# Value projection of a dilated-attention layer: from 384 columns a unit to 512 columns over several units

## The chip, the cores and the metric

The kernel runs on one core of one Trainium2 chip. The metric is the device time of one execution in microseconds (us). The median of three runs is 747.87 us (747.73 to 748.14).

## What is computed

A trunk of two layers on 256 tokens of 1024 features in float32: an even layer (neighbourhood attention and latent attention) with its MLP, then an odd layer with its MLP, and a final norm. The change lies in the odd layer's attention alone. Cut to that:

```python
def odd_mixer(xn, w_in, w_o, cos_f, sin_f):      # xn = rms_norm(x, norm_mix[layer])
    hcat = (xn @ w_in).reshape(b, s, 3, 3, 16, 64)   # group, q/k/v, head, dim
    q = apply_rope(hcat[:, :, :, 0], cos_f, sin_f)
    k = apply_rope(hcat[:, :, :, 1], cos_f, sin_f)
    v = hcat[:, :, :, 2]
    return dilated_attention(q, k, v) @ w_o
```

Each of 16 heads has three groups of queries, keys and values (windows of 128 at stride 1, 512 at stride 4, 2048 at stride 16). A softmax runs over each group, and the three outputs are weighted by their softmax denominators, which is the same as one softmax over all three together.

## The kernel before

**Layout.** A unit is a pair of heads; there are 8. Products keep float32 accuracy by splitting each operand into a high and a low part: `split` (L181, L182) makes the high part on ScalarE and the low part on VectorE, and `mm3` (L185 to L187) multiplies high by high, high by low and low by high. The normed input is kept as `pair` (high and low parts side by side) without the norm's factor rstd; that factor is multiplied in afterwards, into the values as they leave PSUM (L846 to L850) and into the rope tables for queries and keys (L989 to L991).

**Weights.** `specs` lists all weight chunks in the order of use. `weight()` hands out the next one and first calls `prefetch`, which issues loads up to four chunks ahead on SP's queue (L150) and splits up to two chunks ahead, in four pieces each. There are four buffers of raw chunks and three of split ones. The odd layer uses, per unit, three chunks of 2048 columns for queries and keys (`w_oqk`, in `QK_ORDER` 0, 2, 1) and two of 1536 for values (`w_ov`).

**PSUM.** Eight banks: four with the tag "acc" (products) and four with the tag "w" (scores, transposes, row products).

**Queries and keys** (`qk_steps`, L854). Each chunk makes two halves f of 128 columns; each half takes eight pairs of matmuls, one of 512 columns (L867) and one of 256 (L868), in two steps. A chunk is four steps, a unit twelve. What a half leaves in its bank is added up on VectorE (L874 with ScalarE's copy L873, or the reduce L876). `rope` then swaps quarters of the partitions, by DMA on SP's queue for chunks 0 and 2 and by four ScalarE copies (L885, L886) for chunk 1, and multiplies and adds on VectorE (L888 to L898). Chunk 0 gives q and k of the first group (`q0h`, `q0l`), chunk 2 the keys `k12` and chunk 1 the queries `q12` of the other two groups (L894).

**Values** (`value_steps`, L829). For one unit: two token tiles, each one bank of 384 columns, eight k-slices by three matmuls (L185 to L187, called from L844). The first 128 columns are the first group's and leave by VectorE (L846); the others leave by ScalarE in pieces of 64 x 128 (L849, L850), rearranged by tokens.

**Attention** (L912). `scores` fills four "w" banks (L194 for the first group, 16 small matmuls L925 for the others, which read `q12`) and runs the softmax (L934 to L938); `turn` transposes probabilities (L945) and copies them out (L947); `mix` multiplies them by the values (L955, L960) in two banks. `attend` (L974) gives eight steps: scores with the mix of the unit before, four turns, and empty ones.

**Order.** `weave(main, side)` (L196) calls the steps of one list and deals the other list's steps out among them. Tile then orders each engine's instructions from the program, before anything runs. In the opening (L980 to L992) unit 0's values are woven with the squares of x; then `rstd` follows (L244: column sums on TensorE, L239; power on GpSimd, L247), the diagonals of rstd (L258), the evacuations of the values, unit 0's queries and keys in two pieces, and between these pieces the row product (L265) that brings rstd to the rope tables. After that each unit's 12 query-key and 4 value steps are woven with the attention of the unit before. Unit 6's mix is dealt out at the end of unit 7's values (L1002), and unit 7's attention runs beside the output projection.

Of the kernel before, what the change touches and what calls it, by code (L numbers as in the profile page):

```python
# [16 lines left out]
F32 = mybir.dt.float32  # L17
# [6 lines left out]
P = 128  # L24
D = 1024
KT = D // P
# [14 lines left out]
NORM_PRIO = 300  # L41

QK_ORDER = (0, 2, 1)


@with_exitstack
def trunk(ctx, tc, a, out):
# [29 lines left out]
    def bank(tag):  # L77
        return ps.tile([P, 512], F32, tag=tag, name=tag)
# [51 lines left out]
    plan("w_uq", 2 * 768)  # L130
    plan("w_oe", 2 * D)
    plan_mlp(0)
    for u in range(8):
        ov = [(a["w_ov"][u, j], 4 * 384) for j in range(2)]
        oqk = [(a["w_oqk"][u, j], WCH) for j in QK_ORDER]
        specs.extend(oqk + ov if u else ov + oqk)
    plan("w_oo", 2 * D)
    plan_mlp(1)

# [667 lines left out]
    def odd(op, xT, s):  # L807
# [14 lines left out]
        def unit_tiles(u):  # L822
            d = {"k12": k12[u % 2]}
            for n, shape, dt in (("q0h", [P, 2, T], F32R), ("q0l", [P, 2, T], F32R), ("q12", [P, 2, T], F32),
                                 ("v0", [P, NT, P], F32), ("v12", [P, 4, P], F32)):
                d[n] = op.tile(shape, dt, tag=n, name=n, bufs=2)
            return d

        def value_steps(d):  # L829

            wt, acc = [], {}

            def gemm(i, half):
                if len(wt) <= half:
                    wt.append(weight())
                if half == 0:
                    acc[i] = bank("acc")
                pq = acc[i]
                wh, wl = wt[half]
                for k in range(4):  # L840
                    ws = slice(k * 384, k * 384 + 384)
                    kk = 4 * half + k
                    mm3(pq[:, 0:384], xh[:, kk, tok(i)], xl[:, kk, tok(i)], wh[:, ws], wl[:, ws], kk == 0, kk == KT - 1)
            def out(i):  # L844
                pq, ri = acc[i], column(r[0], i)
                nc.vector.tensor_scalar(d["v0"][:, i, :], pq[:, 0:P], ri, None, ALU.mult)  # L846
                for c in range(2):
                    rows = slice(64 * c, 64 * c + 64)
                    nc.scalar.activation(d["v12"][0:64, 2 * i + c, :], pq[rows, P:2 * P], AF.Copy, scale=ri[rows])  # L849
                    nc.scalar.activation(d["v12"][64:P, 2 * i + c, :], pq[rows, 2 * P:3 * P], AF.Copy, scale=ri[rows])  # L850

            return [lambda i=i, h=h: gemm(i, h) for i in range(NT) for h in range(2)], [lambda i=i: out(i) for i in range(NT)]

        def qk_steps(d):  # L854


            hold = {}

            def gemm(b, f, half):
                if f == 0 and half == 0:  # L860
                    hold["w"], hold["q"] = weight(), op.tile([P, 2, T], F32, tag="qk32", name="qk32", bufs=2)
                if half == 0:
                    hold["p"] = bank("acc")
                (wh, wl), pq, q32 = hold["w"], hold["p"], hold["q"]
                for k in range(4 * half, 4 * half + 4):
                    ws = slice((f * KT + k) * P, (f * KT + k + 1) * P)
# [12 lines left out]

            def rope(b, pq):  # L880

                sw, r1 = op.tile([P, 512], F32, tag="swap", name="sw", bufs=2), scratch([2, T], "r1")
                change = nc.scalar.copy if b == 1 else nc.sync.dma_start
                for r in range(0, P, 64):
                    change(sw[r:r + 32], pq[r + 32:r + 64])  # L885
                    change(sw[r + 32:r + 64], pq[r:r + 32])  # L886
                sw = sw.rearrange("p (f n) -> p f n", f=2)
                nc.vector.tensor_tensor(r1, pq.rearrange("p (f n) -> p f n", f=2), cosT.unsqueeze(1).broadcast_to([P, 2, T]), op=ALU.mult)  # L888
                nc.vector.tensor_tensor(sw, sw, sinT.unsqueeze(1).broadcast_to([P, 2, T]), op=ALU.mult)
                if b == 0:  # L890
                    nc.vector.tensor_tensor(r1, r1, sw, op=ALU.add)
                    split(d["q0h"], d["q0l"], r1)
                elif b == 1:
                    nc.vector.tensor_tensor(d["q12"], r1, sw, op=ALU.add)  # L894
                else:
                    for r in (0, 64):
                        cut = lambda z: z[r:r + 64].rearrange("p j (c n) -> p j c n", n=64)
                        nc.vector.tensor_tensor(d["k12"][r:r + 64, :, :, r:r + 64], cut(r1), cut(sw), op=ALU.add)  # L898

            return [lambda v=(b, f, h): gemm(*v) for b in QK_ORDER for f in range(2) for h in range(2)]  # L900

        def all_values(d, prio=0):
            g, o = value_steps(d)
            o = [lambda f=f: early(f) for f in o] if prio else o

            def early(f):
                with tc.high_priority(prio):
                    f()

            return [g[0], lambda: run_all([g[1], o[0]]), g[2], lambda: run_all([g[3], o[1]])]  # L910

        def attention(u, d):  # L912

# [34 lines left out]

            def mix(out_tag):
                pvo = [bank(out_tag) for _ in range(NT)]  # L950
                for i in range(NT):
                    for kk in range(NT):
                        for j in range(2):
                            cs = slice(64 * j, 64 * j + 64)
                            nc.tensor.matmul(pvo[i][cs, 0:P], d["v0"][:, kk, cs], turned[i, j][:, kk, :], start=kk == 0, stop=False)  # L955
                    for c in range(2):
                        qs = slice(64 * c, 64 * c + 64)
                        for j in range(2):
                            cs = slice(64 * j, 64 * j + 64)
                            nc.tensor.matmul(pvo[i][cs, qs], d["v12"][:, 2 * i + c, cs], turned[i, j][:, 2, qs], start=False, stop=c == 1)  # L960
                with tc.high_priority(NORM_PRIO):
                    for i in range(NT):
                        split(*(z[:, u % 4, tok(i)] for z in mixed[u // 4]), pvo[i][:, 0:P])
# [13 lines left out]
            done.append(mix)  # L977
            return [lambda: (scores(), before("acc")), nothing, nothing, t0, t1, nothing, t2, t3]

        d, nd = unit_tiles(0), unit_tiles(1)  # L980
        v0, v_out = value_steps(d)
        squares = square_steps(s)
        weave(v0[0::2] + v0[1::2], squares, 1)
        r = [rstd(s)]
        dg = [diagonal(r[0], t) for t in range(NT)]
        run_all(v_out)
        first = qk_steps(d)
        run_all(first[:2])
        row = as_row(dg)  # L989
        for z in (cosT, sinT):  # L990
            nc.vector.tensor_tensor(z, z, row, op=ALU.mult)  # L991
        run_all(first[2:])  # L992
        weave(qk_steps(nd) + all_values(nd), attend(0, d) + [nothing], 3)
        for u in range(2, 7):
            d, nd = nd, unit_tiles(u)
            weave(qk_steps(nd) + all_values(nd), attend(u - 1, d) + [nothing] * 2)

        d, nd = nd, unit_tiles(7)
        steps = attend(6, d)
        mix = done.pop()  # L1000
        weave(qk_steps(nd) + all_values(nd, NORM_PRIO), steps + [nothing, lambda: mix("w")])
        steps = attend(7, nd)  # L1002
        steps[0]()
        accs, wo = open_accs(), {}
        mix = done.pop()
# [52 lines left out]
def _layout(i):  # L1058
# [20 lines left out]
    d["w_ov"] = f(wo[:, :, 2].reshape(2, 4, P, 3, 8, P).transpose(4, 0, 2, 1, 3, 5).reshape(8, 2, P, 4 * 384))  # L1079
# [34 lines left out]
```

## Time and profile before

| what | value |
|---|---|
| median of three runs | 747.87 us |
| the profiled execution | 748.65 us |
| its span | 746.9 us |
| granted TensorE clock, mean | 0.997 |
| VectorE's split of the raw weights, 512 columns | x408, mean 687 ns |
| the same, 384 columns | x68, mean 553 ns |

The profile is of one execution, and its times are microseconds from the start of the span. Engines: PE is TensorE's matmuls and PEld its weight loads, DVE is VectorE, ACT ScalarE, POOL GpSimd, SP SyncE. L182 is line 182 of the kernel before. A matmul's modelled duration contains its way through the array, so the pitch from one start to the next tells more than the duration. The second layer's attention lies between about 294 and 553 us.

### The profile page before, as it was taken

The page shows a single profiled execution, that of the slowest core. Times are in us where ns is not written, and L with a number is a line of the kernel's source. Part 1 is how long each engine was busy: PE and PEld are TensorE (multiplying, and loading weights), DVE is VectorE, ACT ScalarE, POOL GpSimd, SP SyncE. Part 2 cuts the span into 40 slices and gives each one's busy share as a digit, 9 for nine tenths or more (in the row PEclk, how much of TensorE's full clock was granted, in tenths as well). Part 3 has the DMA queues.
Part 4 walks back from the last instruction along what each step waited for, and adds up shares of the span by engine and source line. Part 5 has one row for each costly group of instructions (what it writes and reads, how often), then busy time and mean ns, then how long its engine had stood idle before and what let it go on. Part 6 is the DMA issues. An engine that isn't in the chain of part 4 may idle for free.

```text
span 746.9 us, 12279 instructions
## 1 busy us (share of the span) xinstructions
PE 739.0 (99%) x4635; PEld 646.4 (87%) x4635; DVE 544.2 (73%) x1137; ACT 484.8 (65%) x1075; POOL 8.7 (1%) x20
## 2 busy tenths in 40 slices
PE   9999999999999999999999999999999999999996
PEld 6998998888888888889899899998998888888885
DVE  6778858766566666997888788888858765665664
ACT  6788967554554555677786877867856554554551
POOL 0100000000000001000000000000000000000000
PEclk9999999999999999999999999999999999999998
DMA  8763334464555545554645636445545555545501
GB/s 282 317 255 114 114 113 170 171 225 173 179 211 177 186 172 165 200 183 165 208 141 178 223 122 215 165 162 198 203 165 176 190 198 197 186 183 187 193 15 56
DMA packets 25163, 133.19 MB, mean 178 GB/s; under 512 B 3728, under 2 KB 4752, under 8 KB 12304
## 3 DMA queue, kind: packets, MB, share of 16 engines
q1 hardware_dynamic: 24960, 132.15, 50.1%
q8 instruction: 36, 0.59, 0.3%
q10 hardware_dynamic: 144, 0.26, 0.1%
q14 instruction: 23, 0.19, 0.1%
HBM read 127.16 MB, written 1.05 MB: 172 GB/s over the span
## 4 chain that ended last, share of the span: by engine, by line
PE 93%; DMA 3%; DVE 1%; issue 1%; SPq 1%; ACT 1%; POOL 0%; POOLq 0%; ACTq 0%
PE w L370 16%; PE acc L185 14%; PE acc L187 13%; PE acc L186 13%; PE acc L867 12%; PE w L371 8%; PE acc L868 6%; PE w L194 1%; PE w L945 1%; PE w L925 1%; PE w L743 1%; DMA gx<-in_gx 1%; DMA bias<-in_rpb 1%; DMA raw<-in_w_v 1%; PE w L757 1%
## 5 line engine op out<-in xcount | busy, mean ns | idle before, releaser
L182 DVE TENSOR_TENSOR wlo<-raw,whi 128x512 fp32r<-128x512 f32 (+3 forms) x487 | 306.6, 664 | 135.1 <-ACT whi L181 134.4
L181 ACT CAST whi<-raw 128x512 fp32r<-128x512 f32 (+3 forms) x487 | 264.3, 601 | 171.3 <-PE w L370 62.3
L370 PE MATMUL w<-pair,whi 128*128 128x512 f32 x512 | 182.2, 397 | 0.0
L371 PE MATMUL w<-pair,wlo 128*128 128x256 f32 x512 | 143.9, 281 | 0.0
L867 PE MATMUL acc<-pair,whi 128*128 128x512 f32 x384 | 139.4, 403 | 0.0
L370 PEld LDWEIGHTS w<-pair,whi 128*128 128x128 f32 x512 | 96.2, 188 | 23.2
L868 PE MATMUL acc<-pair,wlo 128*128 128x256 f32 x384 | 108.1, 282 | 0.0
L185 PE MATMUL acc<-whi,hh 128*128 128x512 f32 x250 | 98.1, 392 | 0.0
L187 PE MATMUL acc<-whi,hl 128*128 128x512 f32 x250 | 97.7, 391 | 0.0
L186 PE MATMUL acc<-wlo,hh 128*128 128x512 f32 x250 | 97.7, 391 | 0.0
L371 PEld LDWEIGHTS w<-pair,wlo 128*128 128x128 f32 x512 | 96.1, 188 | 0.9
L867 PEld LDWEIGHTS acc<-pair,whi 128*128 128x128 f32 x384 | 72.2, 188 | 16.2
L868 PEld LDWEIGHTS acc<-pair,wlo 128*128 128x128 f32 x384 | 72.2, 188 | 0.2 <-issue 0.2
L187 PEld LDWEIGHTS acc<-whi,hl 128*128 128x128 f32 x250 | 47.0, 188 | 9.9
L185 PEld LDWEIGHTS acc<-whi,hh 128*128 128x128 f32 x250 | 47.0, 188 | 9.8
L186 PEld LDWEIGHTS acc<-wlo,hh 128*128 128x128 f32 x250 | 47.0, 188 | 8.9
L185 PE MATMUL acc<-whi,pair 128*128 128x384 f32 x128 | 43.8, 342 | 0.0
L187 PE MATMUL acc<-whi,pair 128*128 128x384 f32 x128 | 43.1, 337 | 0.0
L186 PE MATMUL acc<-wlo,pair 128*128 128x384 f32 x128 | 43.1, 337 | 0.0
L374 ACT COPY side<-w 128x256 f32<-128x256 f32 x64 | 23.7, 370 | 22.1 <-PE w L371 22.1
L375 DVE TENSOR_TENSOR u<-w,side 128x256 f32<-128x256 f32 x64 | 27.0, 421 | 3.8 <-ACT side L374 3.0
L181 ACT CAST hh<-hsq 128x512 fp32r<-128x512 f32 x32 | 19.9, 621 | 10.2 <-DVE hsq L377 10.2
(215 smaller groups left out, 1112.3 us busy)
## 6 DMA issues: line engine op xcount, KB each, us to landing
raw<-in_w SPq DMA_DIRECT2D x64, 1024.0 KB, 4.8
raw<-in_w_oqk SPq DMA_DIRECT2D x24, 1024.0 KB, 5.0
raw<-in_w_ov SPq DMA_DIRECT2D x16, 768.0 KB, 4.4
raw<-in_w_qk SPq DMA_DIRECT2D x4, 1024.0 KB, 8.9
raw<-in_w_oe SPq DMA_DIRECT2D x4, 1024.0 KB, 5.2
sw<-qk SPq DMA_DIRECT2D x64, 64.0 KB, 2.4
raw<-in_w_oo SPq DMA_DIRECT2D x4, 1024.0 KB, 5.1
bias<-in_rpb SPq DMA_DIRECT2D x8, 256.0 KB, 4.2
```

The lines of the kernel that those rows point to most:

```text
L181: a = nc.scalar.copy(hi, src).ins
L182: return a, (eng or nc.vector).tensor_tensor(lo, src, hi.bitcast(F32), op=ALU.subtract).ins
L185: nc.tensor.matmul(o, sh, mh, start=first, stop=False)
L186: nc.tensor.matmul(o, sh, ml, start=False, stop=False)
L187: nc.tensor.matmul(o, sl, mh, start=False, stop=last)
L194: nc.tensor.matmul(o[j], y[pb, 0, ts], z[pb, 1, :], start=n == 0, stop=n == 2)
L370: nc.tensor.matmul(two(pu[f]), w[0][:, c], xT[2][:, k], start=k == 0, stop=False)
L371: nc.tensor.matmul(pu[f][:, 0:T], w[1][:, c], xT[0][:, k, :], start=False, stop=k == KT - 1)
L374: nc.scalar.copy(side[:, f], pu[f][:, T:2 * T])
L375: nc.vector.tensor_tensor(u[:, f], pu[f][:, 0:T], side[:, f], op=ALU.add)
L867: nc.tensor.matmul(two(pq), wh[:, ws], xp[:, k], start=k == 0, stop=False)
L868: nc.tensor.matmul(pq[:, 0:T], wl[:, ws], xh[:, k, :], start=False, stop=k == KT - 1)
```

## The change

Values are made in blocks of 512 columns. A block (b, c) belongs to half b of the units (0 to 3, 4 to 7): c = 0 is the first group's values for all four units, c = 1 and 2 are the other two groups' values for two units each. There are six blocks, each of two token tiles by eight k-slices by three matmuls of 512 columns, in eight steps; each has two weight chunks of 2048 columns. The opening makes blocks (0,0) and (0,1) together, then unit 0's queries and keys. The rest is dealt out by `ODD_PLAN`, one entry beside each unit's attention; the scores of units 1 to 6, with the mix of the unit before, now stand ahead of the entry's first step. Unit 6's mix goes with unit 7's scores. The weights are laid out on the host to fit.

```diff
+def odd_weights():
+    v = lambda b, c: [("w_ov", b, c, h) for h in range(2)]
+    qk = lambda u, js=QK_ORDER: [("w_oqk", u, j) for j in js]
+    out = [p for pair in zip(v(0, 0), v(0, 1)) for p in pair] + qk(0)
...
+ODD_PLAN = ((("qk", 1), ("qk", 2, QK_ORDER[:1])),
+            (("qk", 2, QK_ORDER[1:]), ("v", 0, 2)),
+            (("qk", 3), ("v", 1, 0)),
+            (("qk", 4), ("v", 1, 1)),
+            (("qk", 5), ("qk", 6, QK_ORDER[:1])),
+            (("qk", 6, QK_ORDER[1:]), ("qk", 7, QK_ORDER[:2])),
+            (("qk", 7, QK_ORDER[2:]), ("v", 1, 2)))
...
+        values = {}
+        def value_steps(b, c, prio=NORM_PRIO):
+            hold = {}
+            def gemm(i, k):
+                if i == 0 and k % 4 == 0:
+                    hold["w"] = weight()
+                if k == 0:
+                    hold[i] = bank("acc")
+                wh, wl = hold["w"]
+                for k in (k, k + 1):
+                    ws = slice((k % 4) * 512, (k % 4 + 1) * 512)
+                    mm3(hold[i], xh[:, k, tok(i)], xl[:, k, tok(i)], wh[:, ws], wl[:, ws], k == 0, k == KT - 1)
             def out(i):
...
+                if c == 0:
+                    if i == 0:
+                        values[b, 0] = op.tile([P, NT, 4, P], F32, tag="v0", name="v0", bufs=2)
+                    nc.vector.tensor_scalar(values[b, 0][:, i], pq.rearrange("p (u n) -> p u n", u=4), ri, None, ALU.mult)
+                    return
...
+                for g in range(2):
+                    src = pq[:, 2 * P * g:2 * P * (g + 1)].rearrange("p (u n) -> p u n", u=2)
+                    for h in range(2):
+                        rows = slice(64 * h, 64 * h + 64)
+                        nc.scalar.activation(values[b, c][64 * g:64 * g + 64, :, 2 * i + h, :], src[rows], AF.Copy, scale=ri[rows])
...
+            steps = [[lambda i=i, k=k: gemm(i, k) for k in range(4 * h, 4 * h + 4, 2)] for h in range(2) for i in range(NT)]
...
+        def made_beside(plan, units):
+            out = []
+            for kind, *at in plan:
+                if kind == "v":
+                    g, o = value_steps(*at)
+                    out += g[0] + g[1] + g[2] + [lambda o=o, f=g[3][0]: run_all([o[0], f]), lambda o=o, f=g[3][1]: run_all([f, o[1]])]
...
-        d, nd = unit_tiles(0), unit_tiles(1)
-        v0, v_out = value_steps(d)
+        units = {0: unit_tiles(0)}
+        (g0, o0), (g1, o1) = value_steps(0, 0, 0), value_steps(0, 1, 0)
         squares = square_steps(s)
-        weave(v0[0::2] + v0[1::2], squares, 1)
+        weave([f for h in (0, 2) for g in (g0, g1) for i in range(2) for f in g[h + i]], squares, 1)
         r = [rstd(s)]
         dg = [diagonal(r[0], t) for t in range(NT)]
-        run_all(v_out)
+        run_all(o0 + o1)
...
-        weave(qk_steps(nd) + all_values(nd), attend(0, d) + [nothing], 3)
-        for u in range(2, 7):
-            d, nd = nd, unit_tiles(u)
-            weave(qk_steps(nd) + all_values(nd), attend(u - 1, d) + [nothing] * 2)
-
-        d, nd = nd, unit_tiles(7)
-        steps = attend(6, d)
-        mix = done.pop()
-        weave(qk_steps(nd) + all_values(nd, NORM_PRIO), steps + [nothing, lambda: mix("w")])
-        steps = attend(7, nd)
+        for u in range(7):
+            side = attend(u, units[u])
+            if u == 0:
+                weave(made_beside(ODD_PLAN[u], units), side + [nothing], 3)
+            else:
+                side[0]()
+                weave(made_beside(ODD_PLAN[u], units), side[1:] + [nothing] * 2)
+        steps = attend(7, units[7])
```

## Rows read from the trace of the kernel before

**Rows 1.** The page: busy time of each engine, and the chain by engine
```profile
PE 739.0 (99%) x4635; PEld 646.4 (87%) x4635; DVE 544.2 (73%) x1137; ACT 484.8 (65%) x1075; POOL 8.7 (1%) x20
...
PE 93%; DMA 3%; DVE 1%; issue 1%; SPq 1%; ACT 1%; POOL 0%; POOLq 0%; ACTq 0%
```

**Rows 2.** The chain of waits in order of time: start, us, what; second layer
```profile
382.71 0.90 PE w L194 x11
...
412.73 0.90 PE w L194 x11
```

**Rows 3.** The windows view of 382.7 to 412.7 us
```profile
core 0: us, PE busy (x) PEld busy (x) DVE busy (x) ACT busy (x) POOL busy (x), PEclk, DMA share, GB/s
382.70:412.70 30.00, 30.00 (x219) 27.43 (x218) 24.58 (x55) 23.77 (x55) 0.00 (x0) 1.00 0.52 176
```

**Rows 4.** The timeline, TensorE, 493 to 500 us: start, us, engine, line
```profile
493.25 0.34 PE L187 MATMUL acc<-whi,pair 128*128 128x384 f32 x1
...
499.84 0.34 PE L186 MATMUL acc<-wlo,pair 128*128 128x384 f32 x1
```

**Rows 5.** The timeline, the layer's opening; brackets: idle time before, what ended it
```profile
303.74 0.39 PE L867 MATMUL acc<-pair,whi 128*128 128x512 f32 x1
...
304.79 0.40 PE L867 MATMUL acc<-pair,whi 128*128 128x512 f32 x1
...
305.02 0.50 PE L239 MATMUL w<-mean,squares 128*128 128x1 f32 x4
...
305.38 0.36 PE L868 MATMUL acc<-pair,wlo 128*128 128x256 f32 x1
...
305.80 1.06 POOL L247 TENSOR_TENSOR rstd<-ms,mhalf 128x2 f32<-128x2 f32 x1 [10.09 <-DVE ms L241]
...
306.88 0.28 PE L868 MATMUL acc<-pair,wlo 128*128 128x256 f32 x1
...
307.24 0.71 PE L265 MATMUL w<-diag,mean 128*128 128x128 f32 x4
...
307.71 0.51 PE L867 MATMUL acc<-pair,whi 128*128 128x512 f32 x1
```

**Rows 6.** The timeline, unit 0's third product and scores
```profile
322.23 0.69 DVE L876 TENSOR_REDUCE qk<-acc 128x256 f32<-128x512 f32 x1
...
328.58 0.51 PE L867 MATMUL acc<-pair,whi 128*128 128x512 f32 x1
...
329.33 0.88 PE L925 MATMUL w<-k,q 128*64 128x128 f32 x12 [0.24 <-DVE q L894]
```

**Rows 7.** The timeline, TensorE, the first layer's MLP
```profile
255.83 0.39 PE L185 MATMUL acc<-whi,hh 128*128 128x512 f32 x1
...
258.55 0.39 PE L185 MATMUL acc<-whi,hh 128*128 128x512 f32 x1
```

**Rows 8.** Groups by form, VectorE, 382.7 to 412.7 us: busy, mean ns | idle before
```profile
L182 DVE TENSOR_TENSOR wlo<-raw,whi 128x512 fp32r<-128x512 f32 x14 | 9.3, 687 | 2.3 <-ACT whi L181 2.1
...
L182 DVE TENSOR_TENSOR wlo<-raw,whi 128x384 fp32r<-128x384 f32 x8 | 4.0, 554 | 0.0
...
L889 DVE TENSOR_TENSOR sw<-sw,sinT 128x512 f32<-128x512 f32 x3 | 2.1, 687 | 1.1 <-DMA sw<-qk 1.1
...
L876 DVE TENSOR_REDUCE qk<-acc 128x256 f32<-128x512 f32 x3 | 2.1, 685 | 0.9 <-PE acc L868 0.9
...
L846 DVE TENSOR_SCALAR v<-acc,rstd 128x128 f32<-128x128 f32 x2 | 0.7, 348 | 0.7 <-PE acc L187 0.7
```

**Rows 9.** The timeline, a probability tile and its transposes
```profile
391.38 1.12 ACT L938 ACTIVATE pp<-pp,drz 128x384 f32<-128x384 f32 x2
...
402.51 0.49 PE L945 MATMUL w<-ident,pp 128*128 128x128 f32 x3
```

**Rows 10.** The timeline, TensorE, unit 6's mix and what follows
```profile
529.26 0.66 PE L955 MATMUL w<-pts,v 128*64 128x128 f32 x8
...
530.75 0.44 PE L185 MATMUL acc<-whi,pair 128*128 128x384 f32 x1
```

**Rows 11.** The windows view of the end, columns as in the third group
```profile
740.50:746.90 6.40, 0.38 (x4) 0.17 (x2) 1.80 (x5) 0.72 (x1) 0.67 (x1) 0.69 0.21 82
```

More of the change, by code (lines that the diff above doesn't have):

```diff
@@ L43 @@
 QK_ORDER = (0, 2, 1)
+def odd_weights():
+    v = lambda b, c: [("w_ov", b, c, h) for h in range(2)]
+    qk = lambda u, js=QK_ORDER: [("w_oqk", u, j) for j in js]
+    out = [p for pair in zip(v(0, 0), v(0, 1)) for p in pair] + qk(0)
+    for step in ODD_PLAN:
+        for kind, *at in step:
+            out += v(*at) if kind == "v" else qk(*at)
+    return out
+ODD_PLAN = ((("qk", 1), ("qk", 2, QK_ORDER[:1])),
[5 more added lines that the diff above has]
+            (("qk", 7, QK_ORDER[2:]), ("v", 1, 2)))
 @with_exitstack
@@ L132, in trunk @@
     plan_mlp(0)
[L133 to L136, printed above, removed]
+    for kind, *at in odd_weights():
+        specs.append((a[kind][tuple(at)], WCH))
     plan("w_oo", 2 * D)
@@ L824, in unit_tiles @@
             for n, shape, dt in (("q0h", [P, 2, T], F32R), ("q0l", [P, 2, T], F32R), ("q12", [P, 2, T], F32),
-                                 ("v0", [P, NT, P], F32), ("v12", [P, 4, P], F32)):
+                                 ):
                 d[n] = op.tile(shape, dt, tag=n, name=n, bufs=2)
             return d
[L829 to L843, printed above, removed]
-            def out(i):
[L845 to L852, printed above, removed]
@@ L854, in qk_steps, with early @@
-        def qk_steps(d):
+        values = {}
[10 more added lines that the diff above has]
+                    mm3(hold[i], xh[:, k, tok(i)], xl[:, k, tok(i)], wh[:, ws], wl[:, ws], k == 0, k == KT - 1)
+            def out(i):
+                pq, ri = hold[i], column(r[0], i)
+                if c == 0:
[3 more added lines that the diff above has]
+                    return
+                if i == 0:
+                    values[b, c] = op.tile([P, 2, 4, P], F32, tag="v12", name="v12", bufs=2)
+                for g in range(2):
[3 more added lines that the diff above has]
+                        nc.scalar.activation(values[b, c][64 * g:64 * g + 64, :, 2 * i + h, :], src[rows], AF.Copy, scale=ri[rows])
+            def early(i):
+                with tc.high_priority(prio):
+                    out(i)
+            steps = [[lambda i=i, k=k: gemm(i, k) for k in range(4 * h, 4 * h + 4, 2)] for h in range(2) for i in range(NT)]
+            return steps, [lambda i=i: early(i) for i in range(NT)]
@@ L857, in qk_steps, with values_of @@
+        def values_of(u):
+            b, x = divmod(u, 4)
+            return values[b, 0][:, :, x, :], values[b, 1 + x // 2][:, x % 2]
+        def qk_steps(d, js=QK_ORDER):
             hold = {}
@@ L898, in rope @@
                         nc.vector.tensor_tensor(d["k12"][r:r + 64, :, :, r:r + 64], cut(r1), cut(sw), op=ALU.add)
[L900 to L910, printed above, removed]
+            return [lambda v=(b, f, h): gemm(*v) for b in js for f in range(2) for h in range(2)]
+        def made_beside(plan, units):
[5 more added lines that the diff above has]
+                else:
+                    u, js = at[0], at[1] if len(at) > 1 else QK_ORDER
+                    if u not in units:
+                        units[u] = {}
+                        out.append(lambda u=u: units[u].update(unit_tiles(u)))
+                    steps = qk_steps(units[u], js)
+                    if js[0] == QK_ORDER[0]:
+                        steps[0] = lambda a=out.pop(), b=steps[0]: run_all([a, b])
+                    out += steps
+            return out
         def attention(u, d):
@@ L950, in mix @@
                 pvo = [bank(out_tag) for _ in range(NT)]
+                v0, v12 = values_of(u)
                 for i in range(NT):
@@ L954, in mix @@
                             cs = slice(64 * j, 64 * j + 64)
-                            nc.tensor.matmul(pvo[i][cs, 0:P], d["v0"][:, kk, cs], turned[i, j][:, kk, :], start=kk == 0, stop=False)
+                            nc.tensor.matmul(pvo[i][cs, 0:P], v0[:, kk, cs], turned[i, j][:, kk, :], start=kk == 0, stop=False)
                     for c in range(2):
@@ L959, in mix @@
                             cs = slice(64 * j, 64 * j + 64)
-                            nc.tensor.matmul(pvo[i][cs, qs], d["v12"][:, 2 * i + c, cs], turned[i, j][:, 2, qs], start=False, stop=c == 1)
+                            nc.tensor.matmul(pvo[i][cs, qs], v12[:, 2 * i + c, cs], turned[i, j][:, 2, qs], start=False, stop=c == 1)
                 with tc.high_priority(NORM_PRIO):
@@ L978, in attend @@
             return [lambda: (scores(), before("acc")), nothing, nothing, t0, t1, nothing, t2, t3]
-        d, nd = unit_tiles(0), unit_tiles(1)
-        v0, v_out = value_steps(d)
+        units = {0: unit_tiles(0)}
+        (g0, o0), (g1, o1) = value_steps(0, 0, 0), value_steps(0, 1, 0)
         squares = square_steps(s)
-        weave(v0[0::2] + v0[1::2], squares, 1)
+        weave([f for h in (0, 2) for g in (g0, g1) for i in range(2) for f in g[h + i]], squares, 1)
         r = [rstd(s)]
         dg = [diagonal(r[0], t) for t in range(NT)]
-        run_all(v_out)
-        first = qk_steps(d)
+        run_all(o0 + o1)
+        first = qk_steps(units[0])
         run_all(first[:2])
@@ L992, in odd @@
         run_all(first[2:])
-        weave(qk_steps(nd) + all_values(nd), attend(0, d) + [nothing], 3)
-        for u in range(2, 7):
-            d, nd = nd, unit_tiles(u)
-            weave(qk_steps(nd) + all_values(nd), attend(u - 1, d) + [nothing] * 2)
-        d, nd = nd, unit_tiles(7)
-        steps = attend(6, d)
-        mix = done.pop()
-        weave(qk_steps(nd) + all_values(nd, NORM_PRIO), steps + [nothing, lambda: mix("w")])
-        steps = attend(7, nd)
+        for u in range(7):
+            side = attend(u, units[u])
+            if u == 0:
+                weave(made_beside(ODD_PLAN[u], units), side + [nothing], 3)
+            else:
+                side[0]()
+                weave(made_beside(ODD_PLAN[u], units), side[1:] + [nothing] * 2)
+        steps = attend(7, units[7])
         steps[0]()
@@ L1078, in _layout @@
     d["w_oqk"] = f(qk.transpose(2, 3, 1, 4, 0, 5).reshape(8, 3, P, WCH))
-    d["w_ov"] = f(wo[:, :, 2].reshape(2, 4, P, 3, 8, P).transpose(4, 0, 2, 1, 3, 5).reshape(8, 2, P, 4 * 384))
+    v = wo[:, :, 2].reshape(2, 4, P, 3, 2, 4, P)
+    v0 = v[:, :, :, 0].transpose(3, 0, 2, 1, 4, 5).reshape(2, 1, 2, P, WCH)
+    v12 = v[:, :, :, 1:].reshape(2, 4, P, 2, 2, 2, 2, P).transpose(4, 5, 0, 2, 1, 3, 6, 7).reshape(2, 2, 2, P, WCH)
+    d["w_ov"] = f(np.concatenate([v0, v12], 1))
     d["w1"] = f(i["mlp_w1"].reshape(2, KT, P, 16, 256).transpose(0, 3, 2, 1, 4).reshape(2, 16, P, WCH))
```

## The prediction, made before the change had run

> **What bounds the kernel now.** I began with the page's busy times and its chain [rows 1]: TensorE is busy for 99% of the span and makes 93% of the chain that ended last, while VectorE (73%) and ScalarE (65%) have room. A change can therefore gain only by shortening TensorE's own work or one of its few holes, and lose only by making a new hole. Next the chain of waits in order of time over the second layer's attention [rows 2]: the scores of units 2 and 3 start at 382.71 and 412.73 us. One unit thus takes 30.02 us, and the windows view shows TensorE 30.00 us busy in that stretch [rows 3]: no hole at all. A unit's parts follow from the pitch of the matmuls, not from their modelled duration. In the timeline [rows 4] the 384-column matmuls of the values go from 493.25 to 499.84 in 38 steps, 0.1734 us each; a 512-column and a 256-column matmul of the query-key product take 0.35 us a pair (303.74 to 304.79 is three pairs [rows 5]). A unit is 48 x 0.35 = 16.9 us for queries and keys (5.65 a chunk of weights), 48 x 0.1734 = 8.3 us for values, and 4.8 are left for attention.
>
> The layer's holes are small. In its opening [rows 5] the column sums of the squares start at 305.02, rstd is out at 306.86, and the row product made of it starts at 307.24; TensorE's last matmul ahead of it starts at 306.88 and takes 0.118, so that it waits some 0.25 us. In unit 0's scores [rows 6] the local scores wait for q12: they start 0.75 us after a matmul whose pitch is 0.23 (304.79 to 305.02 [rows 5]), a hole of 0.5.
>
> **The change, part by part.**
>
> *Values in 512 columns.* Before: 8 units x 2 x 8 x 3 = 384 matmuls of 384 columns, 384 x 0.1734 = 66.6 us. After: 6 blocks x 48 = 288 matmuls of 512. The first layer's MLP has the same form, tokens stationary and 512 weight columns moving [rows 7]: 255.83 to 258.55 in 12 steps, 0.2267 us. 288 x 0.2267 = 65.3 us. The columns are the same in all; what goes is 96 times some 13 ns beside them. **-1.28 us**, all on the path. Bounds: 0, if the wide pitch is 0.231, and -1.4.
> Those rows put 13 ns beside the columns of either width (160 and 213 ns at 2.4 GHz, the granted clock being 1.00). The Trainium skill (TensorE: Matmul & The Clock Gate, "Back-to-back issue gap") gives N/2.4 + 2.5 ns; by it the edit would be worth an estimated 96 x 2.5 ns = 0.24 us. The trace's pitch disagrees with it, and the sum goes by the trace.
>
> *Splits and evacuations.* VectorE's half of the value weights' split is 64 pieces of 0.554 us and becomes 48 of 0.687 [rows 8]: 35.4 to 33.0 us. Its 16 evacuations of 0.348 become 4 of 512 columns, about 0.685 each by the reduce that reads as much from PSUM: 5.6 to 2.7. ScalarE's work shrinks in the same way. Both lie beside TensorE: 0 us. Loads bring the same bytes in 36 chunks in place of 40 on the same SP queue: 0, covered by a chunk's 5.65 us.
>
> *The opening.* Here I expect the gain to go. Before, it makes two value accumulators, so two of the four "acc" banks stay free, and the query-key product runs on from 303.74 while the norm is still under way [rows 5]. After, it makes four, for blocks (0,0) and (0,1). All four banks are full when the values end, and each is left only by an evacuation that multiplies by rstd. rstd hangs on a TensorE product, the column sums, which stand behind the weave in the program, and TensorE keeps to the program's order among what is ready: a probability tile left ScalarE at 392.50 and was turned at 402.51, at its place [rows 9]. So the sums come behind the last value matmul, although the squares will be long done, and meanwhile nothing can run but the row product, which has a "w" bank. Priced by [rows 5]: 1.84 us from the sums' start to rstd, 0.4 for the two diagonals ahead in VectorE's order (306.86 to 307.24), 0.685 for the evacuation and 0.1 for the handover, about 3.05. Of it 0.36 (the sums: 305.02 to 305.38), 0.47 (the row product) and the 0.25 of waiting are in the time already. **+1.97 us**. Bounds: -0.25, if the sums slip in earlier, and +2.6, if VectorE has a piece of a split (0.69) in front.
>
> *Unit 0's scores* keep their place, four query-key steps after the last matmul for q12; VectorE and ScalarE can catch up in the opening's hole. I take half of the 0.5: **-0.25** (bounds -0.5 and +0.3).
>
> *Units 1 and 5.* Their scores were 8.3 us of values and a step behind the unit's last query-key matmul. Now four steps lie between, 5.65 us, and 0.9 of scores until q12 is read. In unit 0, the like case, q12 took from 322.23 to about 329.2 [rows 6], 6.95 against 6.55: 0.4 each. I take half for unit 1, which follows as crowded a stretch, and nothing for unit 5: **+0.2** (bounds 0 and +1.0). In the other units 10.9 us of values, or two chunks, lie between: 0.
>
> *Unit 6's mix* stood apart between value steps and took 1.49 us there, 529.26 to 530.75 [rows 10]. Now it goes with unit 7's scores, as in every other unit; its matmuls stay, and one switch out of and into long matmuls is saved, a fraction of those 1.49: **-0.2** (bounds 0 and -0.4). The mix waits for the last values' second evacuation, which has the scores and half a mix as cover.
>
> *Steps of queries and keys alone* (beside units 0, 4 and 5). VectorE is busy for 24.6 us of a unit [rows 3]; without values (4.0 + 0.7 [rows 8]) 19.9, for three chunks and attention. A fourth chunk adds at most a third: 26.5 us against TensorE's 4 x 5.65 + 4.8 = 27.4. It fits: 0 (bounds 0 and +3.3, see the rivals).
>
> Sum: -1.28 + 1.97 - 0.25 + 0.2 - 0.2 = +0.44 us. The profiled execution took 748.65 us (span 746.9 and 1.75 around it), so 749.1 in its terms; it stands 0.78 above the median of the runs, 747.87, and the forecast against that is **748.3 us**.
>
> **The rivals.** A measurement of this kernel can tell a difference of about 0.2%, 1.5 us, from none.
> 1. *The bank wait doesn't come* (0.22): the sums are placed among the values, since the squares are done some 10 us before these end. For it: the order does bend where an operand is expected late (a long matmul stands in the middle of unit 0's scores [rows 6]). Against it: the value matmuls have weights and banks, and stand earlier in the program. Then the gain stands: -1.28 - 0.25 - 0.25 + 0.2 - 0.2 = -1.78, 746.1 us.
> 2. *Slower: VectorE becomes the bound* in the three steps without values (0.11). It works in order and idles 1.1 us a unit for the halves swapped by DMA and 0.9 for TensorE's results [rows 8]. If that stays, 26.5 + 2.0 = 28.5 us against 27.4: 1.1 lost in each, 3.3 in all at the most. The third for a fourth chunk counts attention in, so I take 1.8: 750.1 us. It decides once VectorE's splits are less than a chunk ahead. Against it: its longest idle time, 2.1 us for ScalarE's halves of the split, it has because it is ahead.
> 3. *The clock falls in the hole of the opening* (0.05). A mean granted clock of 0.69 over the last 6.4 us [rows 11] is full speed for 2.4 and half for 4.0 us, so that it fell some 2 us after the last matmul. A hole of 2 us is close to that. With as long at half speed as there, 2.0 us more: 750.3 us.
> 4. *The wider matmul is hardly cheaper* (0.05): a pitch of 0.2303, the columns plus 17 ns, leaves 66.6 - 66.3 = 0.3 of the 1.28 us: 749.3 us. The formula of the Trainium skill cited above comes out there too, by another way.
>
> **How the numbers follow.** The forecast has the other 0.57. Its bounds, not all at one end together, are some 1.3 us on either side, 747.0 to 749.6. Faster by over 0.2% needs less than 746.4: two thirds of rival 1 and a sliver of the forecast, 0.17. Slower needs more than 749.4: most of rivals 2 and 3, some of 4 and a little of the forecast, 0.18. The rest, 0.65, is within. The range goes down to rival 1, with 0.3 to spare, and up to just short of rivals 2 and 3: 745.8 to 749.8.
>
> **What would show it.** In the profile after: 288 value matmuls 0.227 us apart; behind the opening's last one a hole of about 2 us in TensorE, ended by VectorE's first evacuation of v0, with the row product inside it; no hole ahead of a row product later; units 32 to 33 us apart with values for four, 27 to 28 without values; q12's wait under 0.5 us in units 1 and 5; wlo never the releaser of a matmul of this layer. I am wrong if the column sums stand among the value matmuls (rival 1), if matmuls of the layer wait for wlo (rival 2), or if the wide pitch is not 0.227 (rival 4).

## The result, and the profile after

| | before | after |
|---|---|---|
| median | 747.94 us (747.73 to 748.14) | 749.73 us (749.48 to 750.21) |
| profiled execution | 748.65 us | 749.48 us |
| its span | 746.9 us | 747.7 us |
| granted clock, mean | 0.997 | 0.998 |

The ratio is 1.0025, 95% interval 1.0016 to 1.0035: the change made the kernel 1.8 us slower. Little in the page's first rows tells so. TensorE has 96 matmuls fewer and is busy for 1.1 us less than in [rows 1]:

```profile
span 747.7 us, 12005 instructions
...
PE 737.9 (99%) x4539; PEld 633.2 (85%) x4539; DVE 540.1 (72%) x1109; ACT 473.8 (63%) x1027; POOL 8.3 (1%) x20
...
PE 95%; issue 1%; ACT 1%; DVE 1%; DMA 1%; SPq 0%; POOL 0%; POOLq 0%
```

The two spans can't be set against each other as they are: the first loads came at other times, and the layer begins 0.78 us earlier in the profile after. So I took the layer's own length, from the first value matmul to the last matmul of the output projection that is shown. In the timeline of TensorE, before:

```profile
294.54 0.34 PE L185 MATMUL acc<-whi,pair 128*128 128x384 f32 x1
...
559.94 0.28 PE L187 MATMUL acc<-obh,wlo 128*128 128x256 f32 x1
```

and after:

```profile
293.76 0.39 PE L205 MATMUL acc<-whi,pair 128*128 128x512 f32 x1
...
560.70 0.28 PE L207 MATMUL acc<-obh,wlo 128*128 128x256 f32 x1
```

That is 265.40 us before and 266.94 after: **+1.54 us**, all within the layer (the second MLP behind it takes 180.65 us in both). Each matmul of this stretch can be given the time until the next one starts, which adds up to the whole (and 0.12 us for the last one, in both); grouped by kind:

| TensorE's time, us | before | after | difference |
|---|---|---|---|
| values (384, then 288 matmuls) | 67.86 | 67.46 | -0.40 |
| column sums and what follows them idle | 0.36 | 1.84 | +1.48 |
| row product and what follows it | 0.47 | 0.95 | +0.48 |
| output projection | 22.62 | 23.16 | +0.54 |
| queries and keys | 139.33 | 138.96 | -0.37 |
| the rest of attention, tokens' turns | 34.88 | 34.68 | -0.20 |

The opening, where the hole was forecast, in the timeline after (all engines):

```profile
316.39 0.39 PE L207 MATMUL acc<-whi,pair 128*128 128x512 f32 x1
...
316.62 0.50 PE L259 MATMUL w<-mean,squares 128*128 128x1 f32 x4
...
317.40 0.69 POOL L267 TENSOR_TENSOR rstd<-ms,mhalf 128x2 f32<-128x2 f32 x1 [22.47 <-DVE ms L261]
...
318.12 0.48 DVE L278 TENSOR_SCALAR diag<-ident,rstd 128x128 f32<-128x128 f32 x2 [0.80 <-POOL rstd L267]
...
318.46 0.71 PE L285 MATMUL w<-diag,mean 128*128 128x128 f32 x4 [1.34 <-DVE diag L278]
318.52 1.40 DVE L871 TENSOR_SCALAR v<-acc,rstd 128x512 f32<-128x512 f32 x2
319.41 0.47 PE L905 MATMUL acc<-pair,whi 128*128 128x512 f32 x1 [0.24 <-DVE v L871]
```

The last value matmul is followed at once by the sums, and the first query-key matmul starts 2.79 us after them: its releaser, in the brackets, is VectorE's evacuation of v0, which waited for rstd. GpSimd had been idle for 22 us. Against [rows 5] this costs 1.48 + 0.48 us, less the 0.25 us of waiting that the query-key row loses.

Behind it the steady stretch is as quiet as before. The chain of waits shows the scores of units 1 to 6:

```profile
363.32 0.90 PE w L214 x11
390.38 0.91 PE w L214 x9
423.10 0.91 PE w L214 x12
455.83 0.91 PE w L214 x12
483.18 0.91 PE w L214 x12
510.54 0.91 PE w L214 x12
```

27.1, 32.7, 32.7, 27.4 and 27.4 us apart, where [rows 2] had 30.0 throughout. In the windows view VectorE is 92% busy in the most crowded of them, and TensorE has no hole (columns as in the third group of rows):

```profile
455.70:483.10 27.40, 27.40 (x201) 24.03 (x200) 21.80 (x46) 21.62 (x47) 0.00 (x0) 1.00 0.50 168
483.10:510.40 27.30, 27.30 (x201) 24.02 (x200) 25.20 (x53) 19.57 (x43) 0.00 (x0) 1.00 0.48 149
```

Two more places are dear. Unit 0's scores still wait for q12, now 0.82 us from matmul to matmul (0.75 in [rows 6]):

```profile
344.26 0.40 PE L905 MATMUL acc<-pair,whi 128*128 128x512 f32 x1
345.08 1.09 PE L971 MATMUL w<-k,q 128*64 128x128 f32 x16 [0.43 <-DVE q L932]
```

and behind unit 6's mix the output projection waits for a bank that the mix has filled, until its split (`obl` on VectorE) has left it:

```profile
536.54 0.28 PE L207 MATMUL acc<-oah,wlo 128*128 128x256 f32 x1
...
536.89 0.19 PEld L205 LDWEIGHTS acc<-oah,whi 128*128 128x128 f32 x1 [0.28 <-DVE obl L202]
536.90 0.38 PE L205 MATMUL acc<-oah,whi 128*128 128x256 f32 x1
...
537.12 0.28 PE L206 MATMUL acc<-oal,whi 128*128 128x256 f32 x1
...
537.70 0.38 PE L205 MATMUL acc<-oah,whi 128*128 128x256 f32 x1
...
537.92 0.28 PE L206 MATMUL acc<-oal,whi 128*128 128x256 f32 x1
```

### The profile page after: what moved, and what is told of

Its sections match the earlier page's. It is cut to its first block, busy times and chain, and to the rows that moved or that the text cites. A ratio compares the mean times of both kernels' runs of the same rounds, so it can differ in the third digit from the quotient of the medians.

```text
span 747.7 us, 12005 instructions
## 1 busy us (share of the span) xinstructions
PE 737.9 (99%) x4539; PEld 633.2 (85%) x4539; DVE 540.1 (72%) x1109; ACT 473.8 (63%) x1027; POOL 8.3 (1%) x20
## 4 chain that ended last, share of the span: by engine, by line
PE 95%; issue 1%; ACT 1%; DVE 1%; DMA 1%; SPq 0%; POOL 0%; POOLq 0%
PE w L390 16%; PE acc L205 14%; PE acc L207 13%; PE acc L206 13%; PE acc L905 12%; PE w L391 8%; PE acc L906 6%; PE acc L553 2%; PE w L991 1%; PE w L214 1%; PE w L763 1%; PE w L971 1%; PE w L777 1%; DMA raw<-in_w_cv 1%; PE acc L1002 1%
## 5 line engine op out<-in xcount | busy, mean ns | idle before, releaser
L202 DVE TENSOR_TENSOR wlo<-raw,whi 128x512 fp32r<-128x512 f32 (+2 forms) x471 | 304.6, 680 | 128.6 <-ACT whi L201 128.1
L201 ACT CAST whi<-raw 128x512 fp32r<-128x512 f32 (+2 forms) x471 | 262.6, 614 | 178.0 <-PE w L390 62.4
L205 PE MATMUL acc<-whi,pair 128*128 128x512 f32 x96 | 38.6, 402 | 0.0
L207 PE MATMUL acc<-whi,pair 128*128 128x512 f32 x96 | 37.7, 393 | 0.0
L206 PE MATMUL acc<-wlo,pair 128*128 128x512 f32 x96 | 37.4, 389 | 0.0
```

The source lines that it names most:

```text
L201: a = nc.scalar.copy(hi, src).ins
L202: return a, (eng or nc.vector).tensor_tensor(lo, src, hi.bitcast(F32), op=ALU.subtract).ins
L205: nc.tensor.matmul(o, sh, mh, start=first, stop=False)
L206: nc.tensor.matmul(o, sh, ml, start=False, stop=False)
L207: nc.tensor.matmul(o, sl, mh, start=False, stop=last)
```

## The experiments

Medians of one table row are of the same chip; "layer" is the length defined above, from each run's own trace. In the rows "halves of the input apart", "output steps reordered", "unit 0's scores later" and "before, two banks held", the median mixes executions in which TensorE's clock fell and executions in which it did not; they are told apart below. The profiles, and so the layers, of the first and the last of these rows are of executions in which it fell.

| kernel | median, us | ratio to before (95%) | layer, us |
|---|---|---|---|
| sums before the last four value steps | 748.31 | 1.0003 (0.9994 to 1.0011) | 265.52 |
| block (0,1) in "w" banks | 747.92 | 1.0000 (0.9991 to 1.0009) | 265.08 |
| halves of the input apart | 750.66 | 1.0033 (1.0021 to 1.0044) | 268.54 |
| output steps reordered | 749.30 | 1.0021 (1.0011 to 1.0031) | 266.47 |
| unit 0's scores later | 749.76 | 1.0023 (1.0013 to 1.0033) | 266.25 |
| before, two banks held | 751.70 | 1.0050 (1.0036 to 1.0063) | 270.45 |
| value matmuls in two halves | 749.60 | 1.0018 (1.0009 to 1.0027) | 266.87 |
| three repairs | 746.64 | 0.9980 (0.9971 to 0.9988) | 263.90 |
| before, repaired | 747.40 | 0.9991 (0.9982 to 1.0000) | 265.04 |
| three repairs, beside it | 746.63 | 0.9982 (0.9973 to 0.9990) | 263.90 |

**The column sums earlier.**

```diff
-        weave([...16 value steps...], squares, 1)
+        weave(opening[:12], squares, 1)
         r = [rstd(s)]
         dg = [diagonal(r[0], t) for t in range(NT)]
-        run_all(o0 + o1)
+        run_all(o0)
+        run_all(opening[12:])
+        run_all(o1)
```

> The changed kernel, with the column sums, rstd and the diagonals called after 12 of the opening's 16 value steps, and block (0,0) evacuated before the last four. Theory (the four banks wait for rstd, which waits behind the values): the hole of 1.49 + 0.48 us at the opening's end goes, so about 1.7 us come off, 748.0 us, level with the kernel before. Rival (the hole only moves, because VectorE or the split of the next chunk is not ready there, and the loss lies in the wider blocks): the time stays within 0.4 us of 749.7.

This run's timeline of TensorE:

```profile
311.26 0.50 PE L259 MATMUL w<-mean,squares 128*128 128x1 f32 x4
...
316.99 0.39 PE L207 MATMUL acc<-whi,pair 128*128 128x512 f32 x1
317.22 0.39 PE L905 MATMUL acc<-pair,whi 128*128 128x512 f32 x1
```

The sums start at 311.26 in place of 316.62, the first query-key matmul follows the last value matmul by 0.23 us, the row product no longer waits, and the layer loses 1.42 us of its 1.54. In this run unit 0's local scores wait longer for q12 (0.67 us idle in place of 0.43), so that some of the hole comes back there.

**Two more banks.**

```diff
-        (g0, o0), (g1, o1) = value_steps(0, 0, 0), value_steps(0, 1, 0)
+        (g0, o0), (g1, o1) = value_steps(0, 0, 0), value_steps(0, 1, 0, "w")
```

(`value_steps` takes its banks' tag as an argument.)

> The changed kernel, with block (0,1) of the opening in two of the idle w banks; the column sums stay behind the values. Theory of the banks: queries and keys run on while the norm is made, the hole goes, about 748.0 us. Rival (it is the late column sums as such that cost, since they and the row product stand in TensorE's order): at most the first half of the hole goes, 749 us or more.

Here the sums stay where they were, behind the values. This run's timeline, all engines:

```profile
316.92 0.50 PE L259 MATMUL w<-mean,squares 128*128 128x1 f32 x4
...
317.28 0.48 PE L905 MATMUL acc<-pair,whi 128*128 128x512 f32 x1
...
318.82 1.41 DVE L871 TENSOR_SCALAR v<-acc,rstd 128x512 f32<-128x512 f32 x2
```

The query-key product starts 0.36 us behind the sums and 1.5 us ahead of the evacuation that released it before. The layer is 1.86 us shorter. So late sums cost nothing as long as a bank is free: it is the four filled banks, and the two experiments take the hole away from either side.

**The same wait in the kernel before.**

```diff
         v0, v_out = value_steps(d)
+        held = [bank("acc") for _ in range(2)]
+        for z in held:
+            nc.tensor.matmul(z[:, 0:P], ident, ident, start=True, stop=True)
...
         dg = [diagonal(r[0], t) for t in range(NT)]
+        for z in held:
+            nc.vector.tensor_scalar(work.tile([P, P], F32, tag="held", name="held"), z[:, 0:P], column(r[0], 0), None, ALU.mult)
```

> The kernel before, with two of its four acc banks taken through the opening: two transposing matmuls of 0.1 us fill them, and two VectorE instructions that multiply by rstd empty them. Nothing else of the change. Theory of the banks: query-key matmuls that ran from 303.7 us on cannot start before rstd (306.9) and the first evacuation; the sums and the row product still run, so a hole of 2.5 to 3.5 us, 750.5 to 751.5 us. Rival (banks are not what held the changed kernel's opening): within 0.5 us of the kernel before.

The median is 3.6 us over that of the kernel before on the same chip (748.12), just past the theory's upper end. But the profiled execution holds a second thing. Its timeline and, under it, the windows view of the same stretch:

```profile
302.95 0.34 PE L187 MATMUL acc<-whi,pair 128*128 128x384 f32 x1
303.77 0.61 PE L239 MATMUL w<-mean,squares 128*128 128x1 f32 x4 [0.49 <-DVE squares L232]
306.10 1.22 PE L265 MATMUL w<-diag,mean 128*128 128x128 f32 x4 [1.72 <-DVE diag L258]
306.98 0.77 PE L867 MATMUL acc<-pair,whi 128*128 128x512 f32 x1
```

```profile
303.20:307.00 3.80, 1.59 (x10) 1.42 (x9) 3.12 (x11) 2.18 (x4) 1.07 (x1) 0.77 0.66 239
307.00:312.00 5.00, 5.00 (x17) 4.25 (x17) 2.84 (x7) 2.91 (x8) 0.00 (x0) 0.50 0.45 190
312.00:316.00 4.00, 4.00 (x24) 3.48 (x23) 1.85 (x4) 1.27 (x3) 0.00 (x0) 0.99 0.28 70
```

TensorE ran the sums alone between 303.3 and 306.1, and its granted clock fell: 0.77 on average over the stretch of the hole, then 0.50, which is 1.2 GHz, for the 5 us behind. That is the rival of the falling clock, in another kernel. Of the four executions two have a mean clock of 0.994 and 0.995 and took 753.04 and 752.24 us, the others 0.998 and 751.09 and 751.17: the hole alone costs some 3 us and the clock 1 to 2 more when it falls. In the changed kernel's ten executions the mean clock is 0.997 or 0.998 and the times lie within 0.8 us: no sign of a fall, with a hole over a quarter shorter (2.79 us from the end of the values to the first query-key matmul, 3.86 here). But that hole is long enough. Three of the versions below keep the changed kernel's opening as it is (halves apart, output steps reordered, unit 0's scores later), and in 10 of their 22 executions the mean clock is 0.996 or 0.997 and the time 1 to 2.3 us longer; one of the ten was profiled and shows the fall behind the hole. The 65 executions of the versions without the hole show no such group. Why the ten of the changed kernel itself were spared isn't shown.

**How wide a matmul pays.**

```diff
                 for k in (k, k + 1):
-                    mm3(hold[i], ..., wh[:, ws], wl[:, ws], k == 0, k == KT - 1)
+                    for h in range(2):
+                        ws = slice((k % 4) * 512 + h * 256, (k % 4) * 512 + h * 256 + 256)
+                        mm3(hold[i][:, h * 256:h * 256 + 256], ..., wh[:, ws], wl[:, ws], (k, h) == (0, 0), (k, h) == (KT - 1, 1))
```

> The changed kernel with block (0,1) in the w banks, and each value matmul of 512 columns made as two of 256, so 576 matmuls for 288. If about 13 ns stand beside the columns of a matmul whatever its width, as the prediction had it, 288 x 13 ns = 3.7 us more than without: 751.7 us. If the time beside the columns grows with the width (256-column matmuls of the output projection have a pitch of 113 to 118 ns, 7 to 11 beside 106.7), the pitch is about 115 and the cost 0 to 1 us: 748 to 749 us; widening from 384 to 512 then had little to save in the first place.

Neither. The layer is 1.79 us longer than with the w banks alone (266.87 against 265.08), the values' row 69.27 us in place of 67.47: 288 more matmuls cost 1.80 us, 6.3 ns each, not 13. The time beside the columns is partly a matmul's own and partly grows with its width. By that price 96 fewer matmuls are worth 0.6 us, and 0.6 is what the pitch in the profile after gives (0.2291 on average, the switches into and out of the blocks left out, in place of 0.2267). In that profile's timeline of TensorE, 24 steps of 0.2288:

```profile
300.14 0.39 PE L205 MATMUL acc<-whi,pair 128*128 128x512 f32 x1
...
305.63 0.39 PE L205 MATMUL acc<-whi,pair 128*128 128x512 f32 x1
```

**Where the operands lie.**

```diff
-        z = act.tile([P, KT, 2, T], F32R, tag="pair", name="pair", bufs=1)
-        return z[:, :, 0, :], z[:, :, 1, :], z
+        z = act.tile([P, 2, KT, T], F32R, tag="pair", name="pair", bufs=1)
+        return z[:, 0], z[:, 1], z.rearrange("p h k n -> p k h n")
```

> The changed kernel, with the normed input's high and low halves in two separate stretches of its tile in place of side by side, in every layer. The wide value matmuls measured 0.2291 us a piece where the MLP's measured 0.2267. If the place of the stationary tokens against the moving weights sets that, their pitch changes, to 0.2267 at best: 288 x 2.4 ns = 0.7 us less, 749.0. If the input's address plays no part, the pitch stays at 0.229 and the time at 749.7. The moving side of the query-key product changes too, which measured 0.353 us a pair: each ns there is 0.4 us.

The value pitch stayed at 0.2292 us, so the stationary side's place isn't the reason; why this pitch lies above the MLP's stays open. The query-key row took 140.47 us in place of 138.96, nearly all of the 1.6 us by which the layer grew, and this looks like the price of a moving side that is now two stretches of 256. It is the clock: in this profile it fell behind the hole of the opening. The windows view, columns as in the third group of rows:

```profile
316.60:319.40 2.80, 1.22 (x10) 0.97 (x8) 1.51 (x5) 1.96 (x5) 0.69 (x1) 1.00 0.70 293
319.40:322.00 2.60, 2.60 (x11) 2.25 (x12) 1.71 (x4) 2.55 (x7) 0.00 (x0) 0.67 0.00 0
322.00:324.00 2.00, 2.00 (x9) 1.67 (x7) 1.29 (x2) 0.60 (x3) 0.00 (x0) 0.57 0.00 0
324.00:330.00 6.00, 6.00 (x36) 5.22 (x35) 4.34 (x8) 3.42 (x7) 0.00 (x0) 1.00 0.53 184
```

A query-key pair took 0.64 us there; behind 325 us the pairs average 0.3594 us in this profile and 0.3595 in that of the changed kernel. Of the six executions three have a mean clock of 0.996 and took 750.93 to 751.19 us, the other three, at 0.997 and 0.998, 749.60 to 750.40, about the changed kernel's time. So the layout cost nothing that these runs show.

**The order of the output projection.**

```diff
-        weave([f for k in range(6) for f in out_steps(accs, mixed, wo, k)], steps[1:] + ...)
+        outs = [out_steps(accs, mixed, wo, k) for k in range(6)]
+        outs = [outs[0][0], outs[1][0], outs[0][1], outs[1][1]] + [f for o in outs[2:] for f in o]
+        weave(outs, steps[1:] + ...)
```

> The changed kernel, with the first four steps of the output projection in the order k0 low, k1 low, k0 high, k1 high. Theory: the wait of 0.24 us behind unit 6's mix, for the bank that its split has to leave, goes: 749.5 us, and no gap there in TensorE's row. Rival (the projection's 0.54 us over the kernel before has another source): the 0.3 us beside that wait stay, and the time is 749.7.

The projection took 22.69 us in place of 23.16, 0.07 over the kernel before, and the layer 266.47. The wait seen as 0.24 us was worth 0.47: the first matmul behind it, and the one that enters the mix's other bank (537.70), have a pitch of 0.22 us in place of 0.11, and both return to 0.11 in this run. Five of the eight executions took 748.89 to 749.37 us at a clock of 0.998, the other three 750.03 to 751.24 at 0.996 or 0.997; the profile is of one of the five.

**Unit 0's scores later.**

```diff
-                weave(made_beside(ODD_PLAN[u], units), side + [nothing], 3)
+                weave(made_beside(ODD_PLAN[u], units), side + [nothing], 5)
```

> The changed kernel, with unit 0's scores two query-key steps later (six after q12's last matmul in place of four). Theory: the wait of 0.6 us for q12 and the block broken around it (1.0 us over the calm units' in all) are the cost of standing too early, and go: 0.6 to 1.0 us less, 748.9. Rival (VectorE is behind after the opening, so that the wait comes back elsewhere): 749.7.

The layer is 0.69 us shorter (266.25). The median, 749.76, doesn't show it, because it stands between two groups of executions: four at a mean clock of 0.999 took 748.76 to 749.09 us, four at 0.996 or 0.997 took 750.43 to 751.09. The profile is of the first group, which lies 0.7 us over the kernel before on the same chip, where the changed kernel lay 1.8 over it.

**The repairs together, and for the kernel before.** The w banks, the output projection's new order and unit 0's later scores stand in one kernel:

> The changed kernel with three repairs: block (0,1) in the w banks, the output projection's first four steps reordered, unit 0's scores two steps later. If the three holes are separate (1.86, 0.47 and 0.6 to 1.0 us of the layer's length), 2.9 to 3.3 us less than the changed kernel and 1.2 to 1.5 less than the kernel before: 746.5 us. If they stand in for one another (VectorE late in each), 747.5 us or more.

The holes are separate: 266.94 - 263.90 = 3.04 us in the layer, and 1.86 + 0.47 + 0.69 is 3.02. The median is 746.64, a ratio of 0.9980 (0.9971 to 0.9988): faster than the kernel before, by 1.5 us, and so than the changed kernel. Is that the change's merit or the repairs'? The kernel before with what fits it:

```diff
-        run_all(first[:2])
+        run_all(first[:3])
         row = as_row(dg)
...
-        weave(qk_steps(nd) + all_values(nd), attend(0, d) + [nothing], 3)
+        weave(qk_steps(nd) + all_values(nd), attend(0, d) + [nothing], 5)
```

> The kernel before with the two repairs that fit it: unit 0's scores two steps later, and the row product one query-key step later. It has values of 384 columns, dealt out as they were. Theory (the wide values and their dealing are worth some 0.4 to 0.7 us of TensorE's time, and the rest of the repaired kernel's lead is repairs): 0.7 to 0.9 us less than the kernel before in the layer, 264.6 against 265.4 and against 263.9 of the version with all three repairs. Rival (the repairs do nothing for the old arrangement, and the whole lead belongs to the wide values): 265.4 in the layer, the time of the kernel before.

> The version with all three repairs again, on the same chip as the repaired kernel before: 0.5 to 1.0 us less than that one, 1.2 to 1.5 less than the kernel before.

The repaired kernel before has 265.04 us, 0.36 under the original where I expected 0.8: with the scores later, a later turn waits for the softmax (0.29 us idle):

```profile
337.35 0.28 PE L868 MATMUL acc<-pair,wlo 128*128 128x256 f32 x1
337.92 0.55 PE L945 MATMUL w<-ident,pp 128*128 128x128 f32 x3 [0.29 <-ACT pp L938]
```

The changed kernel with its repairs leads it by 1.14 us in the layer and by 0.77 in the medians. By rows, 0.40 of the 1.14 lie in the values, 0.63 in queries and keys and 0.18 in attention, less 0.07 in the projection. So the wide values and their dealing are worth up to about 1 us once they stand clear of the banks, the width itself 0.4 of it; part of the rest is the wait that the repair put into the kernel before, so this comparison doesn't settle what the dealing alone is worth.

## Why the prediction was right or wrong

The range, 745.8 to 749.8, held the time (749.73) by 0.07 us, which is luck: its upper end was set just short of rivals 2 and 3, and neither made the loss. The forecast of 748.3 called it no change, +0.4 us over the median that was known, and it was +1.8, clear of the noise (95% interval 1.0016 to 1.0035). What failed are two terms, the values' gain and the price of unit 6's mix, and with them a smaller one, the gain at unit 0's scores. By its steps:

- **The opening** was right, in mechanism and in size. Forecast: +1.97 us, a hole behind the last value matmul, ended by the first evacuation of v0, with the row product inside it. Measured: 1.48 + 0.48 us in the two rows, less the 0.25 of waiting that goes elsewhere, 1.71. GpSimd's power took 0.69 us here and 1.06 in [rows 5], which is more than the difference. (The forecast's parts add up to 3.03 and not 3.05 us.) Two experiments removed it and one made it in the kernel before.
- **The values** are the first term that failed: "-1.28 us", from a pitch of 0.2267 us read off 12 steps of a quiet stretch of the MLP [rows 7]. All 512-column matmuls of that MLP between 140 and 290 us average 0.2280, the switches left out, and the values came at 0.2291: 384 x 0.1734 - 288 x 0.2291 = 0.6 us. With the switches into and out of the blocks the row shows 0.40. Rival 4 had the cause (the wide matmul hardly cheaper, 0.2303) and was nearer than the forecast. The trace agrees with neither number for the time beside the columns: by the Trainium skill's 2.5 ns (TensorE: Matmul & The Clock Gate, "Back-to-back issue gap", where it is the gap of an isolated matmul) the gain would be an estimated 0.24, by the 13 ns of my reading 1.28; halving the width showed 6.3 ns a matmul.
- **Unit 0's scores**: "I take half of the 0.5" as a gain. The wait went from 0.75 to 0.82 us, no gain. The idle time in it is 0.43 us, 0.54 in the version with the w banks, which has no hole in the opening, and 0.24 in the kernel before: the hole let VectorE catch up by some 0.1 us only, and why q12 is later than before stays open. Placing the scores two steps later gave 0.69.
- **Units 1 and 5** were forecast at +0.2 and cost nothing: q12 was there before their scores reached it (362.5 against 364.15 in unit 1, 482.8 against 484.02 in unit 5).
- **Unit 6's mix** is the other term that failed: "-0.2", "which has the scores and half a mix as cover". I followed what the mix waits for and not who waits for the mix: its two "acc" banks are next the output projection's, and they came late, which cost 0.47 us, as the reordered projection shows. The sum has no term for it; the switch that was to be saved can't be told apart in the rows.
- **The steps without values** cost nothing, as forecast; rival 2 (VectorE the bound) is refuted by TensorE's full rows at 25.2 us of VectorE in 27.3.
- **Rival 1** did not come: the sums stood behind the values. **Rival 3**, the clock, did not come in the ten executions here, but it did in 10 of 22 of versions with the same hole, as well as with a longer one. Its mechanism was right, and 0.05 was too low for a kernel with this opening; the fall cost 1.5 us in the query-key row of the one such profile, where it was priced at 2.0.

By the rows of the layer, the values are 0.88 us dearer than forecast (-0.40 for -1.28), the projection 0.54 (nothing was forecast) and the opening 0.26 cheaper (+1.71 for +1.97). The rest of the query-key and attention rows gave -0.32, where the three small terms (-0.25, +0.2, -0.2) make -0.25: their sum came out by luck, for two of the three did not come as forecast. That is the 1.1 us between the sum (+0.44) and the layer (+1.54). The 0.25 us between the layer and the medians' difference of 1.79 lie ahead of the layer or in the spread; nothing here settles which.

## What to carry to other kernels

When work is batched so that more accumulators are open at once, count the banks at the moment the batch ends and ask what each needs in order to leave: here all four hung on a norm whose first matmul stood behind the batch. Either leave a bank to the next product, or call the norm before the batch ends. And read a pitch from a long stretch, not from a calm dozen of steps: a term made of 288 pitches turns an error of 2 ns into half of its gain. Last, before two traces are compared, look at the granted clock in each: one fall of 3.4 us would have passed for the price of a layout here.

## What the runs showed of the hardware that I had not expected

The time a matmul takes beside its columns is no constant: in these runs 117.8 ns on average for 256 columns (11 beside 106.7, the switches left out), 173.4 for 384 (13), 229.1 for 512 (16), with the same stationary tokens, and laying the operands out differently did not change the last. And one short hole was enough for the clock, in some executions of a program and not in others. With two banks held in the kernel before, TensorE ran little but the four sums for 2.8 us; the granted clock halved in the profiled execution, the mean clock and the time say that it did in a second of the four, and the other two show no fall. The query-key pair took 0.64 us in place of 0.353 until the clock came back, 5 us behind the hole. With the opening of the changed kernel, where 2.79 us hold the four sums and the row product, the profile with the halves apart shows it at half speed from 320.3 to 323.7 us, when the query-key matmuls were already running again.
